# One more held pair in each down product, a longer allowance for the weights behind a norm, norm pieces by list, first loads on two queues

## The chip, the cores and the metric

The kernel runs on one core of a Trainium2 chip. The metric is the device time of one execution, in microseconds (us). The engines are named as in the profile: PE multiplies matrices, DVE works on vectors, ACT casts and evaluates functions, POOL is the general one, SP issues most of the DMAs. PEld is the loading of weights into PE.

## The reference, cut to what matters

A single decoder layer for 256 tokens of width 2048, in float32:

```
h = layer_norm(alpha*h + 0.5*swiglu(h, w_ffn1_gu, w_ffn1_down))     # norm 1
... = split(h @ w_in)          # retention, attention, gates
h = layer_norm(alpha*h + mixed @ w_mix_out)                         # norm 2
h = layer_norm(alpha*h + 0.5*swiglu(h, w_ffn2_gu, w_ffn2_down))     # norm 3
h = layer_norm(alpha*h + sigmoid(h @ w_ple_gate) * (p @ w_ple_proj))

swiglu(x, w_gu, w_down): g, u = split(x @ w_gu);  (silu(g) * u) @ w_down
```

The inner width of swiglu is 5632. A layer_norm needs the sum over a whole row, so no product behind a norm can start on a token before the product ahead of it has finished for that token in all 2048 columns.

## The kernel before

**Numbers.** Each float32 operand is carried as two parts that PE multiplies fast: a high part, which ACT casts (L93), and a low part, which DVE gets by subtraction (L94). A product is three matmuls: low × high, high × high, high × low (L302 to L304).

**Weights.** A weight arrives in chunks of 512 KB: a raw load by SP (L109), a high part on ACT, a low part on DVE. `plan` lists all units (one chunk, or two for a scheme with seven products in place of eight) in the order of use. `fill` (L188) is called whenever a unit is done: it makes the next loaded unit if the ready ones amount to less than `ahead` (a sum of the units' times) and there are slots, and asks for the next load if all of it is below `far`. `quiet(True)` stops the making, not the loading. `slots_for_weights` sets slots, `ahead` and `far`. 46 slots of 4 KB for each partition are shared with everything else.

**The order.** The program runs the first feed-forward block f1 (`ffn`, L762), norm 1, the mixers (L975), norm 2, the second feed-forward block f2, norm 3, the embedding (L1337) and the last norm. Each engine does its instructions in the order in which the code writes them. A feed-forward block has gate and up products, and then the down product in two halves of 1024 columns each, d0 and d1.

**What is held back.** The two token halves t = 0 and t = 1 of 128 tokens each are normalised one after the other. So that PE has work meanwhile, the last pairs of chunks ahead of a norm are held back (`HELD_PAIRS`, 2 for f1 and 3 for f2; `HELD_MIX` 4 chunks ahead of norm 2). `held_out` (L433) first runs t = 0 of all held steps (a pair is two steps, one for each 512 columns; a step is six matmuls for each t), then `normal(0)`, which DVE works on while PE runs t = 1 of the same steps, in half-steps of three matmuls. In the last `calm` steps of the t = 0 pass, and after it, `fill` is quiet. Ahead of norm 1 two blocks of w_pp follow (`put_by`, L646), ahead of norm 2 two more; of those a count is six matmuls.

**The norm.** `Norm` (L528): `columns(t, n)` adds a product to the residual (L911) and takes its statistics (L541); `normal(t)` does that for the last 512 columns, works out mean and deviation, and normalises the first 512 columns in two halves (L512, L513); `more(t, c)` normalises piece c of 512 columns. `turn(t, c)` asks for `more(t, c+1)`, unless that is the piece `put_off`, and has PE transpose piece c (L520), ACT cast it and DVE subtract: this gives `ht`, the input of the next product. The lists of events, like

```
events = ((8, (0, 0)), (10, (0, 1)), (11, (0, 2)), (12, "make"), (12, "make"), (12, "sums"))
```

say after how many half-steps of t = 1 a piece (t, c) is turned, a unit is made, or `normal(1)` is done ("sums"). After the norm `first` (L604) does the same for the next product: t = 0 of its first `FRONT` chunks (w_rv behind norm 1, w_pg behind norm 3; `FRONT_PAIRS` pairs of gate and up chunks behind norm 2), then t = 1, with events that turn the pieces of t = 1 and do the put-off one ("more"), and end the quiet ("go").

**The start.** `warm_up` (L1504) has PE transpose an identity 16 times while the first loads come. `load_x_chunk(0)` (L1474) loads the first quarter of x in three pieces and the first two units in two pieces each, all on SP's queue.

Of the kernel before, what the change touches and what calls it, by code (L numbers as in the profile page):

```python
# [23 lines left out]
LN_EPS = 1e-5  # L24
GN_EPS = 1e-5
KD = D // P
# [2 lines left out]

HELD_MIX = 4  # L30
FRONT = 6

WARM = 16
FRONT_PAIRS = 3
HELD_PAIRS = 2, 3
SLOTS = 46


# [12 lines left out]
def layer(ctx: ExitStack, tc: tile.TileContext, io):  # L51
# [44 lines left out]
    class Chunk:  # L96


        def __init__(self, key, pieces=1, queue=None, between=None):
            src = chunk_of(key)  # L100
            self.key, self.paired = key, key[0].endswith("_gu") or key[0][-1] == "2"
            self.name = "_".join(map(str, key))
            self.raw = slot(list(src.shape), F32, "r" + self.name)
            n = src.shape[2] // pieces
            self.parts = [slice(j * n, j * n + n) for j in range(pieces)]
            for j, at in enumerate(self.parts):
                if between is not None and j:
                    between()
                (queue or sync).dma_start(self.raw[:, :, at], src[:, :, at])  # L109

        def make_hi(self):
# [416 lines left out]
    class Norm:  # L528
# [23 lines left out]

        def turn(self, t, c):

            args = self.y, t, self.i, self.new
            if c < 3 and (t, c + 1) != self.put_off:
                self.more(t, c + 1)
            if c == 0:
                for k0 in (0, 2):
                    ln_turn(*args, k0, 2, self.keep.get(c))  # L560
            else:
                ln_turn(*args, 4 * c, 4, self.keep.get(c))

        def follow(self, n, events):

# [196 lines left out]
    def ffn(name, i, ht, norm, keep, residual, keepers, away):  # L762
# [28 lines left out]
        for j in range(KF // 4):  # L791
            pg, pu = banks(f"{name}g{j}"), banks(f"{name}u{j}")
            units = gu_units(j)
            plain = len(units) - sum(kind == "S" for kind, p in units)
            n_of = {(0, 0): KD, (0, 1): KD, (1, 0): KD, (1, 1): KD}
            for kind, p in units:
                if kind == "S":
                    for at in ((0, 0), (0, 1), (1, 0)):
                        n_of[at] -= 1
                    n_of[1, 1] -= 2  # L800
            sums = [[Sum((pg, pu)[n][t], n_of[t, n]) for n in range(2)] for t in range(2)]
            got = []

            if norm is not None and j == 0:
                front, units = units[:FRONT_PAIRS], units[FRONT_PAIRS:]
                steps = [(gu_keys(name, 0)(n, p), 2 * p, n) for _, p in front for n in range(2)]
                norm.first(steps, rhs, sums, (
                    (3, (1, 0)), (5, (1, 1)), (6, "more"), (7, (0, 2)), (8, (1, 2)), (9, (0, 3)), (10, (1, 3)), (10, "go"),
                ))
                slots_for_weights(24)  # L810

            def before(u, j=j, offset=KD // 2 - len(units)):
                u += offset
                if j == 0 and norm is None and u % 2 == 0:
                    first_chunk(u // 2)
                    if u == 6:
                        slots_for_weights(24)
                    if u == 2:
                        load_constants()
                if j == 0 and u == 7:  # L820
                    for g in sorted({p // 2 for p in SEVEN}):
                        hi, lo = (slot([P, 8, P], F32R, f"{name}f{w}{g}") for w in "hl")
                        made[g] = seven_forms(keep[g], hi, lo)
                if j == KF // 4 - 1 and u in (4, 6):
                    convert(u // 2 - 2)

            block(f"{name}{j}", units, gu_keys(name, j), rhs, forms, sums, lambda *a: got.extend(seven_common(*a)), before)
            if got:
                g, v = got
                for x, ps in ((g, pg), (v, pu)):  # L830
                    for t in range(2):
                        dve.tensor_tensor(x[:, t], x[:, t], ps[t], ALU.add)  # L832
                act.activation(g, g, AF.Silu)  # L833
                dve.tensor_tensor(v, g, v, ALU.mult)
            else:
                v = slot([P, 2, 512], F32, f"{name}v{j}")
                for t in range(2):
                    act.activation(v[:, t], pg[t], AF.Silu)
                for t in range(2):
                    dve.tensor_tensor(v[:, t], v[:, t], pu[t], ALU.mult)  # L840
            later(2, lambda j=j, v=v: turned(j, v))
# [44 lines left out]
            block_stats(stats, y, n)  # L886


        last_ahead = 136
        last = {}  # L890
        for at, (kind, p) in enumerate(second + [("P", p) for p in held]):
            last[p // 2] = at
# [11 lines left out]
        pt_ = [banks(f"{name}e{t}") for t in range(2)]  # L904
        sums = [[Sum(pt_[t][n], n_of[1][t, n]) for n in range(2)] for t in range(2)]
        block(f"{name}d1", second, down_keys(name, 1), lhs, forms, sums, fold(1), before_unit)
        slots_for_weights(27, last_ahead, last_ahead + 24)
        steps = [(down_keys(name, 1)(n, p), 2 * p, n) for n in range(2) for p in held]

        def combine(sl, p):  # L910
# [1 line left out]

        norm = Norm((2, 3), sums, combine, y, stats, i, 4 * LN_EPS, keepers, away, (0, 3))
        if i < 2:
            events = ((8, (0, 0)), (10, (0, 1)), (11, (0, 2)), (12, "make"), (12, "make"), (12, "sums"))
            norm.run(steps, lhs, events, (0, 1), 4)
        else:
            norm.run(steps, lhs, ((8, (0, 0)), (11, (0, 1))))
        return norm


# [53 lines left out]
    def mixers(ht, norm, residual, keepers, away):  # L975
# [353 lines left out]
            done(u)  # L1329
            run_side()  # L1330
        steps = [(("w_mix", 3, c), 2 * c, 0) for c in range(first, KD // 2)]
        norm = Norm((3,), sums, combine, y, stats, 1, LN_EPS, keepers, away, (0, 2))
        norm.run(steps, lhs, ((8, (0, 0)), (10, (0, 1)), (10, "sums")), (2, 3))
        return norm

# [1 line left out]
    def embedding(ht, norm, y):  # L1337
# [77 lines left out]
        for blk in range(4):  # L1415
            pgs = banks(f"pg{blk}")
            sums = [Sum(b, KD) for b in pgs]
            sg = slot([P, 2, 512], F32, f"sg{blk}")
            key = ("w_pg", blk)
            if blk == 0:  # L1420
                for j in range(4):
                    pp[j] = load_columns(pp, j, "ppr")
                steps = [(key + (c,), 2 * c, 0) for c in range(FRONT)]
                norm.first(steps, lhs, [[s] for s in sums], (
                    (1, (0, 2)), (1, "sums"), (6, (1, 0)), (7, (1, 1)), (8, (1, 2)), (8, "more"), (9, (1, 3)),
                    (10, (0, 3)), (10, "go"),
                ))
                slots_for_weights(24)
                for c in range(FRONT, KD // 2):
                    u = take(key + (c,))  # L1430
                    tokens_chunk(u.chunk, 2 * c, lhs, sums, (0, 1))
                    done(u)
            elif blk < 3:
                for c in range(KD // 2):
                    u = take(key + (c,))
                    tokens_chunk(u.chunk, 2 * c, lhs, sums, (0, 1))
                    done(u)
                    run_side()
            if blk < 3:
                finish(blk, pgs[0], sg, 0)  # L1440
                later(1, lambda blk=blk, pgs=pgs, sg=sg: finish(blk, pgs[1], sg, 1))
                if blk == 0:
                    g, b = ln_vectors(3)
                    two_rows = small.tile([P, 96], F32, tag="plnm", bufs=1, name="plnm")
                    pool.memset(two_rows, 0.0)
                    ident_r = small.tile([P, P], F32R, tag="identr", bufs=1, name="identr")
                    act.copy(ident_r, ident)
                if blk == 1:
                    later(3, rows_of_vectors)
                    later(4, lambda: scale(0))  # L1450
                    later(6, lambda: scale(1))
                if blk == 2:
                    later(6, lambda: scale(2))
                continue

            def first_done():
                finish(3, pgs[0], sg, 0)
                first_half(*ln_stats(stats[:, 0], 3, 0, LN_EPS))

            steps = [(key + (c,), 2 * c, 0) for c in range(KD // 2)]  # L1460
            held_out(steps, lhs, [[s] for s in sums], lambda t, j: None, first_done, lambda n: None, 0)
            last_half()
# [11 lines left out]
    def load_x_chunk(c):  # L1474
# [4 lines left out]
            split_x(c, slice(0, 4))  # L1479
            return  # L1480
        parts = [slice(0, 1), slice(1, 2), slice(2, 4)]
        load = lambda at: sync.dma_start(raw[:, at], io["xT"][c][:, at])
        load(parts[0])
        for j in range(2):
            u = plan.pop(0)
            u.load(pieces=2, queue=sync, between=lambda: load(parts[1]) if j == 0 else None)
            u.chunk.make_hi()
            room["used"] += u.keeps
            ready.append(u)
        load(parts[2])  # L1490
        first, second = (u.chunk for u in ready)
        split_x(c, parts[0])
        first.make_part(first.parts[0])
# [134 lines left out]
```

## Time and profile before

| | |
|---|---|
| median of 3 runs | 2289.36 us (2289.07 to 2289.7) |
| profiled execution, its own time | 2290.82 us |
| span of that execution | 2288.6 us |
| mean granted TensorE clock | 0.998 |
| ACT busy | 1189.9 us (52%) |
| DMA | 465.88 MB, mean 204 GB/s |

The span runs from the first to the last instruction. A line of the timeline has the start in us, the duration, the engine with the line of the code, the operation, output and inputs, sizes, and how many instructions it stands for (x4); in brackets the idle time of the engine ahead of it and what ended that. A matmul's duration covers its passage through the array; the pace is the distance between starts.

### The profile page before, as it was taken

Reading aid. Unit: us, or ns where it says so; the run is one execution under the profiler, and the core shown is the slowest. Engines: PE = TensorE matmul, PEld = TensorE weight load, DVE = VectorE, ACT = ScalarE, POOL = GpSimd, SP = SyncE. Lnnn points to the kernel's source line nnn. Section 1 sums busy time; section 2 is a strip of 40 time slices with the busy share of each in tenths; the row PEclk is TensorE's granted clock in tenths of the full one; section 3 lists DMA queues with packets and bytes.
Section 4 is the critical chain, followed back from the end, with each engine's and each line's share of the span. In section 5 each row is a group of like instructions: output and inputs, shape, how many; then the busy total and the mean of one; then the engine's idle time right before and its main releaser. Section 6 shows DMA issues by size and latency. Waiting matters only on the chain.

```text
span 2288.6 us, 28866 instructions
## 1 busy us (share of the span) xinstructions
PE 2273.1 (99%) x10492; PEld 1887.0 (82%) x10492; DVE 1948.2 (85%) x2474; ACT 1189.9 (52%) x1438; POOL 97.0 (4%) x56
## 2 busy tenths in 40 slices
PE   9999999999999999999999999999999999999998
PEld 8888888888888888888778888888888888888876
DVE  6999999999988885677789786779999999889877
ACT  5555555556554342435556454355565555555533
POOL 0000000000000530124000000000000000000000
PEclk9999999999999999999999999999999999999999
DMA  8666665665577565545447567566656566565772
GB/s 298 202 204 196 199 210 178 209 198 193 215 280 282 175 224 164 171 161 166 138 152 244 170 218 279 191 226 207 195 191 205 184 203 217 179 221 193 276 258 74
DMA packets 194022, 465.88 MB, mean 204 GB/s; under 512 B 14796, under 2 KB 16460, under 8 KB 193880
## 3 DMA queue, kind: packets, MB, share of 16 engines
q1 hardware_dynamic: 192296, 461.73, 60.9%
q10 hardware_dynamic: 1584, 2.31, 0.4%
q8 instruction: 82, 1.34, 0.2%
q14 instruction: 60, 0.49, 0.1%
HBM read 455.60 MB, written 8.39 MB: 203 GB/s over the span
## 4 chain that ended last, share of the span: by engine, by line
PE 97%; DVE 2%; DMA 0%; issue 0%; ACT 0%; SPq 0%; ACTq 0%
PE f1g L302 3%; PE f1g L304 3%; PE f1g L303 3%; PE f2g L304 3%; PE f2g L302 3%; PE f2g L303 3%; PE rqk L253 3%; PE f1u L304 2%; PE f1u L302 2%; PE f1u L303 2%; PE f2u L304 2%; PE f2u L302 2%; PE f2u L303 2%; PE aqk L253 2%; PE f1d L302 2%; PE f2d L302 2%
## 5 line engine op out<-in xcount | busy, mean ns | idle before, releaser
L94 DVE TENSOR_TENSOR lf_gu<-rf_gu,hf_gu 128x1024 fp32r<-128x1024 f32 (+1 forms) x284 | 334.4, 1211 | 16.2 <-ACT hf_gu L93 15.4
L93 ACT CAST hf_gu<-rf_gu 128x1024 fp32r<-128x1024 f32 (+1 forms) x284 | 282.2, 1043 | 22.3 <-DMA rf_gu<-in_f_gu 20.5
L94 DVE TENSOR_TENSOR lw_in_f<-rw_in_f,hw_in_f 128x1024 fp32r<-128x1024 f32 x140 | 195.6, 1427 | 29.4 <-ACT hw_in_f L93 26.9
L94 DVE TENSOR_TENSOR lf_down<-rf_down,hf_down 128x1024 fp32r<-128x1024 f32 x152 | 181.1, 1220 | 23.1 <-ACT hf_down L93 20.3
L93 ACT CAST hf_down<-rf_down 128x1024 fp32r<-128x1024 f32 x152 | 155.4, 1050 | 75.8 <-DMA rf_down<-in_f_down 21.9
L93 ACT CAST huf_gu<-uf_gu 128x1024 fp32r<-128x1024 f32 x70 | 73.8, 1054 | 156.4 <-DVE uf_gu L168 153.5
L93 ACT CAST hw_in_f<-rw_in_f 128x1024 fp32r<-128x1024 f32 x140 | 138.8, 1051 | 3.2 <-DMA rw_in_f<-in_w_in_f 2.9
L302 PE MATMUL f1g<-hf_gu,xt 128*128 128x512 f32 x247 | 97.2, 393 | 0.5 <-ACT hf_gu L93 0.5
L304 PE MATMUL f1g<-lf_gu,xt 128*128 128x512 f32 x247 | 96.9, 392 | 0.0
L303 PE MATMUL f1g<-hf_gu,xt 128*128 128x512 f32 x247 | 96.9, 392 | 0.0
L302 PE MATMUL f2g<-hf_gu,ht 128*128 128x512 f32 x247 | 96.4, 390 | 0.0
L304 PE MATMUL f2g<-lf_gu,ht 128*128 128x512 f32 x247 | 96.2, 390 | 0.0
L303 PE MATMUL f2g<-hf_gu,ht 128*128 128x512 f32 x247 | 96.2, 389 | 0.0
L93 ACT CAST hvf_gu<-vf_gu 128x1024 fp32r<-128x1024 f32 x70 | 73.8, 1054 | 30.2 <-DVE vf_gu L170 29.5
L833 ACT ACTIVATE eve<-eve 128x1024 f32<-128x1024 f32 x20 | 21.2, 1062 | 124.5 <-DVE eve L832 124.5
L94 DVE TENSOR_TENSOR luf_gu<-uf_gu,huf_gu 128x1024 fp32r<-128x1024 f32 x70 | 85.3, 1218 | 0.0
L94 DVE TENSOR_TENSOR lvf_gu<-vf_gu,hvf_gu 128x1024 fp32r<-128x1024 f32 x70 | 85.3, 1218 | 0.0
L302 PE MATMUL f2u<-hf_gu,ht 128*128 128x512 f32 x212 | 83.8, 395 | 0.0
L302 PE MATMUL f1u<-hf_gu,xt 128*128 128x512 f32 x212 | 83.4, 394 | 0.0
L304 PE MATMUL f2u<-lf_gu,ht 128*128 128x512 f32 x212 | 82.6, 390 | 0.0
L303 PE MATMUL f2u<-hf_gu,ht 128*128 128x512 f32 x212 | 82.6, 390 | 0.0
L303 PE MATMUL f1u<-hf_gu,xt 128*128 128x512 f32 x212 | 82.6, 390 | 0.0
(1358 smaller groups left out, 6452.5 us busy)
## 6 DMA issues: line engine op xcount, KB each, us to landing
rf_gu<-in_f_gu SPq DMA_DIRECT2D x350, 512.0 KB
rf_down<-in_f_down SPq DMA_DIRECT2D x176, 512.0 KB
rw_in_f<-in_w_in_f SPq DMA_DIRECT2D x148, 512.0 KB
rw_rv<-in_w_rv SPq DMA_DIRECT2D x32, 512.0 KB
rw_ret<-in_w_ret SPq DMA_DIRECT2D x32, 512.0 KB
rw_mix<-in_w_mix SPq DMA_DIRECT2D x32, 512.0 KB
rw_pg<-in_w_pg SPq DMA_DIRECT2D x32, 512.0 KB
rw_att<-in_w_att SPq DMA_DIRECT2D x16, 512.0 KB
```

Source lines behind the costliest of these rows:

```text
L93: act.copy(dst_hi, src)
L94: (lo_engine or dve).tensor_tensor(dst_lo, src, dst_hi, ALU.subtract)
L253: pe.matmul(ps[f], hi[:, kk, f * P : (f + 1) * P], rhs(k), start=k == 0, stop=k == n_k - 1,)
L302: pe.matmul(o, al, bh, start=first, stop=False)
L303: pe.matmul(o, ah, bh, start=False, stop=False)
L304: pe.matmul(o, ah, bl, start=False, stop=self.left == 0)
L833: act.activation(g, g, AF.Silu)
```

## The change

- `HELD_PAIRS` goes from 2, 3 to 3, 4: f1 and f2 hold back one pair more ahead of norms 1 and 3, and the events are counted anew. Piece (0,2) of norm 3 and its "sums" move from the embedding's list to the end of the held steps.
- The allowance `last_ahead` behind a down product goes from 136 to 160 (f1) and 150 (f2), with `far` 24 above it as before, and the slots from 27 to 30.
- Behind norm 3, five chunks of w_pg (`FRONT_LAST`) instead of six run by halves.
- Norm 2 puts off no piece; "more" leaves its list. In norms with a put-off piece, `turn(1, 0)` writes `more(1, 1)` behind the transposes and parts of (1,0) instead of ahead of them.
- 19 warm transposes instead of 16; the three loads of x are issued first on SP's queue, the first unit's two loads on ACT's queue, the second unit's on SP's.

```
-WARM = 16
+FRONT_LAST = 5
+WARM = 19
-HELD_PAIRS = 2, 3
+HELD_PAIRS = 3, 4
...
-        def __init__(self, key, pieces=1, queue=None, between=None):
+        def __init__(self, key, pieces=1, queue=None):
...
-            for j, at in enumerate(self.parts):
-                if between is not None and j:
-                    between()
+            for at in self.parts:
                 (queue or sync).dma_start(self.raw[:, :, at], src[:, :, at])
...
         def turn(self, t, c):
             args = self.y, t, self.i, self.new
-            if c < 3 and (t, c + 1) != self.put_off:
+            at_once = (t, c) == (1, 0) and self.put_off is not None
+            following = c < 3 and (t, c + 1) != self.put_off
+            if following and not at_once:
                 self.more(t, c + 1)
             if c == 0:
                 for k0 in (0, 2):
                     ln_turn(*args, k0, 2, self.keep.get(c))
             else:
                 ln_turn(*args, 4 * c, 4, self.keep.get(c))
+            if following and at_once:
+                self.more(t, c + 1)
...
-                    (3, (1, 0)), (5, (1, 1)), (6, "more"), (7, (0, 2)), (8, (1, 2)), (9, (0, 3)), (10, (1, 3)), (10, "go"),
+                    (3, (1, 0)), (5, (1, 1)), (7, (0, 2)), (8, (1, 2)), (9, (0, 3)), (10, (1, 3)), (10, "go"),
...
-        last_ahead = 136
+        last_ahead = 160 if i < 2 else 150
...
-        slots_for_weights(27, last_ahead, last_ahead + 24)
+        slots_for_weights(30, last_ahead, last_ahead + 24)
...
-            events = ((8, (0, 0)), (10, (0, 1)), (11, (0, 2)), (12, "make"), (12, "make"), (12, "sums"))
+            events = ((11, (0, 0)), (13, (0, 1)), (15, (0, 2)), (15, "make"), (15, "make"), (15, "sums"))
             norm.run(steps, lhs, events, (0, 1), 4)
         else:
-            norm.run(steps, lhs, ((8, (0, 0)), (11, (0, 1))))
+            norm.run(steps, lhs, ((10, (0, 0)), (13, (0, 1)), (16, (0, 2)), (16, "sums")))
...
-        norm = Norm((3,), sums, combine, y, stats, 1, LN_EPS, keepers, away, (0, 2))
+        norm = Norm((3,), sums, combine, y, stats, 1, LN_EPS, keepers, away, None)
...
-                steps = [(key + (c,), 2 * c, 0) for c in range(FRONT)]
+                steps = [(key + (c,), 2 * c, 0) for c in range(FRONT_LAST)]
                 norm.first(steps, lhs, [[s] for s in sums], (
-                    (1, (0, 2)), (1, "sums"), (6, (1, 0)), (7, (1, 1)), (8, (1, 2)), (8, "more"), (9, (1, 3)),
-                    (10, (0, 3)), (10, "go"),
+                    (5, (1, 0)), (6, (1, 1)), (7, (1, 2)), (7, "more"), (8, (1, 3)), (9, (0, 3)), (9, "go"),
                 ))
...
-        load = lambda at: sync.dma_start(raw[:, at], io["xT"][c][:, at])
-        load(parts[0])
-        for j in range(2):
+        for at in parts:
+            sync.dma_start(raw[:, at], io["xT"][c][:, at])
+        for queue in (act, sync):
             u = plan.pop(0)
-            u.load(pieces=2, queue=sync, between=lambda: load(parts[1]) if j == 0 else None)
+            u.load(pieces=2, queue=queue)
...
-        load(parts[2])
```

More of the change, by code (lines that the diff above doesn't have):

```diff
@@ L1422, in embedding @@
                     pp[j] = load_columns(pp, j, "ppr")
-                steps = [(key + (c,), 2 * c, 0) for c in range(FRONT)]
+                steps = [(key + (c,), 2 * c, 0) for c in range(FRONT_LAST)]
                 norm.first(steps, lhs, [[s] for s in sums], (
-                    (1, (0, 2)), (1, "sums"), (6, (1, 0)), (7, (1, 1)), (8, (1, 2)), (8, "more"), (9, (1, 3)),
-                    (10, (0, 3)), (10, "go"),
+                    (5, (1, 0)), (6, (1, 1)), (7, (1, 2)), (7, "more"), (8, (1, 3)), (9, (0, 3)), (9, "go"),
                 ))
                 slots_for_weights(24)
-                for c in range(FRONT, KD // 2):
+                for c in range(FRONT_LAST, KD // 2):
                     u = take(key + (c,))
```

## Prediction

> **What bounds the kernel now.** I read the page's head first, then the waits of PE, then the timelines around the three norms and the start.
>
> ```profile
> span 2288.6 us, 28866 instructions
> PE 2273.1 (99%) x10492; PEld 1887.0 (82%) x10492; DVE 1948.2 (85%) x2474; ACT 1189.9 (52%) x1438; POOL 97.0 (4%) x56
> ```
>
> PE is busy for all but 15.5 us of the span. The matmuls, PE's work, are the same in number after the change, so only idle time of PE, and time at a lower clock, can come or go.
>
> ```profile
> PE lnps L520 <- DVE f2y L513: 1.7, 2, 1.2
> PE pg L302 <- DVE ht L94: 1.1, 1, 1.1
> PE lnps L520 <- DVE mixy L513: 1.1, 2, 0.8
> PE lnps L520 <- DVE f1y L513: 0.8, 2, 0.5
> PE f1g L302 <- ACT hf_gu L93: 0.5, 1, 0.5
> ```
>
> The columns are total us, times, longest. Those five are what the change can reach: 5.2 us, nearly all of it PE waiting for DVE to normalise a piece (L512, L513) that PE then transposes (L520). The end of the kernel is not touched. Beside these waits stands a stretch at half clock:
>
> ```profile
> 717.00:720.40 3.40, 2.63 (x14) 1.73 (x14) 3.29 (x8) 0.74 (x2) 0.00 (x0) 1.00 0.96 365
> 2177.25:2180.66 3.41, 1.76 (x10) 1.05 (x9) 3.17 (x10) 0.53 (x2) 0.00 (x0) 1.00 0.94 310
> 2180.66:2184.07 3.41, 3.41 (x11) 2.52 (x10) 3.37 (x6) 0.21 (x1) 0.00 (x0) 0.50 1.03 419
> ```
>
> These are stretches of the windows view: length, busy time of PE, weight load, DVE, ACT, POOL, then granted clock. After a window in which PE was busy 1.76 of 3.41 us the clock was 0.50 for the next; after one with 2.63 it was not.
>
> **Where the numbers stand.** The profiled execution took 2290.82 us, 2.2 beyond its span, and lies 1.46 above the median of the runs, 2289.36. The sum is made against the profiled execution and carried over to the median.
>
> **Norm 1** (f1's down product, three pairs held back where there were two).
>
> ```profile
> 683.14 1.23 DVE L94 TENSOR_TENSOR lf_down<-rf_down,hf_down 128x1024 fp32r<-128x1024 f32 x1 [0.40 <-ACT hf_down L93]
> 691.74 4.62 DVE L94 TENSOR_TENSOR lw_rv<-rw_rv,hw_rv 128x1024 fp32r<-128x1024 f32 x4
> 696.28 0.68 DVE L94 TENSOR_TENSOR pt<-praw,pt 128x512 fp32r<-128x512 f32 x1
> 696.88 0.68 DVE L911 TENSOR_TENSOR f1y<-f1y,f1e 128x512 f32<-128x512 f32 x1
> 702.29 0.48 DVE L513 SCALAR_TENSOR_TENSOR f1y<-f1y,rstd,ln_b 128x256 f32<-128x256 f32 x1
> 703.21 0.48 DVE L513 SCALAR_TENSOR_TENSOR f1y<-f1y,rstd,ln_b 128x256 f32<-128x256 f32 x1
> 705.71 0.75 DVE L513 SCALAR_TENSOR_TENSOR f1y<-f1y,rstd,ln_b 128x512 f32<-128x512 f32 x1
> 698.17 0.39 PE L302 MATMUL f1e<-hf_down,f1al 128*128 128x512 f32 x1
> 703.61 0.60 PE L520 MATMUL lnps<-ident,f1y 128*128 128x128 f32 x4
> 718.62 0.41 PE L520 MATMUL lnps<-ident,f1y 128*128 128x128 f32 x2 [0.51 <-DVE f1y L513]
> 719.17 0.75 DVE L513 SCALAR_TENSOR_TENSOR f1y<-f1y,rstd,ln_b 128x512 f32<-128x512 f32 x1
> 719.84 0.75 DVE L94 TENSOR_TENSOR ht<-lnps,ht 128x256 fp32r<-128x256 f32 x2
> 720.26 0.60 PE L520 MATMUL lnps<-ident,f1y 128*128 128x128 f32 x4
> ```
>
> PE. The first token half of all held chunks runs, then the second. 24 matmuls start from 698.17 to 703.61, 0.2267 us each. One more pair is two more steps. Their 24 matmuls leave the plain part, and 12 come back in the first half, so the first half ends 12 × 0.2267 = 2.72 us sooner: the second half starts at 698.17 − 2.72 = 695.45 and the first piece, due after 33 of its matmuls, at 695.45 + 7.48 = 702.93.
>
> DVE. It works without a gap from 683.14. In the order of the changed program six low parts of w_rv (not four) and pt stand before the first L911: steps 1 and 2 of six are no longer quiet, and the larger allowance lets two more units be made. Each takes 4.62 / 4 less the overlap, 1.135, so the first L911 comes at 696.88 + 2.27 = 699.15; loads asked for sooner can close at most the 0.40 us before 683.14, and I take all of it: 698.75. In before, piece (0,0) was ready in two halves, at 702.77 and 703.69, which is 5.89 and 6.81 after the first L911. So they come at 704.64 and 705.56. With the 0.13 and 0.06 us from ready to start that the rows at norm 3 below show, PE goes on at 704.77, 1.84 late, and after 0.19 of transposes waits 0.66 more: **2.5**. Bounds: 0 if the lows are made in time, 2.9 with nothing of the 0.40 regained.
>
> Piece (0,1) is asked for 9 matmuls later (2.04 and 0.2 for the transposes); DVE has the columns of the second half and its two L512/L513 before it, 706.46 − 703.69 = 2.77 in before. 2.77 + 0.1 against 2.4 gives **0.45**. Then nothing is late until the second half's norm, where 0.8 was waited in two pieces before and is again. What is new there: the list puts L512/L513 of piece (1,1) behind both lows of (1,0), where before they stood ahead of them (719.17 before 719.84). The lows wait for transposes that start at 718.62 and for ACT, and end at 719.84 + 0.75 = 720.59 at the earliest; 1.53 behind them is 722.1 where PE came at 720.26. Two transposes of cover are taken off, and the delay of the lows in before was the pieces ahead of them, so they start some 0.8 sooner: **1.0** (0 to 1.9).
>
> The three make **+3.95**. At norm 3 below, 1.40 and 0.58 late were 1.24 and 0.42 of idle, so 2.5 late is some 2.2 of idle within 2.6 us. A window of 3.4 us that holds it all has PE busy for 1.2, below the 1.76 after which the clock was 0.50. At half clock 3.4 us hold 8 matmuls at 0.427 and lose 8 × 0.2 = 1.6; the 0.45 of piece (0,1) is hidden in it. So **+1.15** more. The windows go on whatever PE does, so a wait of 2.2 can also be cut in two: then no window falls below 1.76. I take it as whole, since 1.7 of it is one wait; both are kept.
>
> A rule speaks against the halving. The Trainium skill, "TensorE: Matmul & The Clock Gate", section "HAM oscillation — how this bites in real kernels", gives the rule as "no PE-idle gaps >~3.4µs"; by it no wait here would halve the clock, and the term would be 0. The trace differs: the longest idle in the window before the halving was 1.2 us. The case without it is rival B.
>
> **Norm 2** (no piece put off).
>
> ```profile
> 1478.87 0.69 DVE L94 TENSOR_TENSOR ht<-keep,ht 128x512 fp32r<-128x512 f32 x1 [2.73 <-ACT ht L93]
> 1492.07 0.66 PE L520 MATMUL lnps<-ident,mixy 128*128 128x128 f32 x4 [0.79 <-DVE mixy L513]
> ```
>
> The L512/L513 of piece (0,2), 1.5 us, move from just before 1492.07 into DVE's 2.73 idle before 1478.87. The wait of 0.79, 0.95 counted from start to start, goes; the next piece was already normalised. **−0.95** (0 if ACT is late).
>
> **Norm 3** (four pairs; five chunks of w_pg in front instead of six).
>
> ```profile
> 2167.48 3.49 DVE L94 TENSOR_TENSOR lw_pg<-rw_pg,hw_pg 128x1024 fp32r<-128x1024 f32 x3
> 2172.19 1.23 DVE L94 TENSOR_TENSOR lw_pg<-rw_pg,hw_pg 128x1024 fp32r<-128x1024 f32 x1 [1.22 <-ACT hw_pg L93]
> 2173.34 0.68 DVE L911 TENSOR_TENSOR f2y<-f2y,f2e 128x512 f32<-128x512 f32 x1
> 2179.49 0.48 DVE L513 SCALAR_TENSOR_TENSOR f2y<-f2y,rstd,ln_b 128x256 f32<-128x256 f32 x1
> 2172.36 0.39 PE L302 MATMUL f2e<-hf_down,f2al 128*128 128x512 f32 x1
> 2177.57 0.39 PE L304 MATMUL f2e<-lf_down,f2ah 128*128 128x512 f32 x1
> 2179.20 0.41 PE L520 MATMUL lnps<-ident,f2y 128*128 128x128 f32 x2 [1.24 <-DVE f2y L513]
> 2180.03 0.44 PE L520 MATMUL lnps<-ident,f2y 128*128 128x128 f32 x2 [0.42 <-DVE f2y L513]
> ```
>
> The sixth low of w_pg, which waited 1.22 for its load, no longer stands before the norm: the first L911 comes at 2170.9, 2.44 sooner, and the last quarter of (0,0) at 2179.97 − 2.44 = 2177.53. PE's second half starts at 2172.36 − 2.72 = 2169.64 and asks after 30 matmuls, at 2176.44: 0.32 + 0.66 = 0.98 of waiting, against 1.40 + 0.58 before, and too little to halve the clock. Before: 1.98 + 1.6 at half clock + 1.28 (the wait on ht) = 4.86. After: 0.98, 0.5 at (0,1) as in norm 1, 0.95 on ht, 0.35 at (1,1), whose pieces now stand behind the lows, and 1.0 for the sixth chunk, made only when the last piece is turned, with one step (6 matmuls, 1.36) to cover the ACT cast and the 1.23 of the low (0.4 to 1.2): 3.78. **−1.1** (−3.9 if nothing is late, +0.5 if the clock halves).
>
> **Start.**
>
> ```profile
> 2.80:6.20 3.40, 2.90 (x13) 2.34 (x11) 1.10 (x3) 1.33 (x3) 0.00 (x0) 1.00 0.89 274
> 1.18 0.42 SPq L109 DMA_DIRECT2D rf_gu<-in_f_gu  x1
> 2.03 0.20 ACT L1513 ACTIVATE warm<-warm 128x1 f32<-128x1 f32 x1
> 5.54 0.80 PE L302 MATMUL f1g<-hf_gu,xt 128*128 128x512 f32 x1 [0.50 <-ACT hf_gu L93]
> 12.00 1.23 DVE L94 TENSOR_TENSOR lf_gu<-rf_gu,hf_gu 128x1024 fp32r<-128x1024 f32 x1 [1.24 <-ACT hf_gu L93]
> 13.54 0.39 PE L304 MATMUL f1g<-lf_gu,xt 128*128 128x512 f32 x1
> 20.66 0.39 ACTq L680 DMA_DIRECT2D cst<-in_cst  x1
> ```
>
> The first chunk's two loads go to ACT's queue, behind the ACTIVATE that ends at 2.23, so up to 1.05 later than 1.18; SP's later loads move up two issues of 0.42. Three more warm transposes fill the 0.50 gap ahead of 5.54. Worst: first matmul 1.05 later at half clock, +0.9. Best: the gap closed, a half-clock window of 1 us less, but the matmul at 13.54 needs the low that ends at 13.23, 0.3 before it: −0.8. I take **0**, between them, since the cast of the first chunk waits for its DMA and not for an issue.
>
> The Trainium skill, "DMA: Bandwidth & Descriptors", section "Issuing engines are not separate DMA queues", says that loads issued by two engines share the same 16 DMA engines and only the issue time is gained. By it the gain is at most those issues; the trace of before cannot show it.
>
> **Sum.** 3.95 + 1.15 − 0.95 − 1.1 + 0 = +3.05: the profiled execution comes to 2293.9, the median to **2292.4**. The loads asked for sooner I cost at nothing: matmuls on chunks that are already made hide them. The DMA share is 0.94 to 1.03 in the windows above, so if one lands late for that, the price is a wait like the 1.22 at 2172.19.
>
> **Rivals.** About 0.2%, 4.6 us, is what a measurement of this kernel can tell from no change: 2284.8 to 2293.9.
> - **A, forecast**, 42%: 2292.4.
> - **B**, the same without the halving at norm 1, 16%: 2291.2. For it: 2.63 of 3.40 did not halve. Against: 1.7 of idle in one wait.
> - **C**, DVE in time at norm 1, because the lows are made before the fold at 686.83 instead of behind it, 14%: the waits of (0,0) and (0,1) go, 1.0 stays: 1.0 − 0.95 − 1.1 = −1.05, 2288.3. Against: DVE has no gap there to make them in.
> - **D**, slower, 20%: the second half of norm 1 halves the clock too. Before, its window had 2.63 of 3.40; 1.0 more idle brings it to about 1.65, just below 1.76, the point from which it decides. Price 1.6, and up to 1.2 for the same at norm 3: 2294.0 to 2295.2, middle 2294.6.
> - **E**, faster, 8%: the change does what a longer second half would, all pieces in time at norm 3 (−3.9), start −0.8, norm 2 −0.95, norm 1 +1.0: 2284.7.
>
> The range takes in A, B, D and the lower side of C: 2287.0 to 2295.3; E and the upper edge of D stay out. Faster 0.07 (E, part), slower 0.21 (D and a tail of A), same 0.72.
>
> **What would show it.** Norm 1: a wait of about 2 us at L520 for f1y, six lows of w_rv ahead of the first L911 at about 699, a new wait of 1 us at (1,1), clock 0.50 once. Norm 2: one wait left, 0.3. Norm 3: no half clock, first L911 at about 2171 on before's scale, waits of PE on ht and on lw_pg. The prediction is wrong if f1y keeps a wait of 0.8 or if DVE has a gap before norm 1.

## The result and the profile after

The changed kernel takes 2297.52 us (median of 6 runs, 2296.95 to 2298.77); the kernel before took 2289.27 beside it. The ratio is 1.0037, with a 95% interval of 1.0025 to 1.005: slower, by 8.2 us. The forecast was 2292.4, and its range ended at 2295.3.

The head of the page, and the waits of PE (total us, times, longest):

```profile
span 2295.0 us, 28860 instructions
PE 2274.3 (99%) x10495; PEld 1885.3 (82%) x10495; DVE 1948.9 (85%) x2474; ACT 1191.0 (52%) x1438; POOL 97.3 (4%) x56
```

```profile
PE lnps L519 <- DVE f1y L512: 7.3, 5, 5.4
PE lnps L519 <- DVE f2y L512: 1.2, 4, 0.4
PE pg L301 <- DVE ht L95: 0.7, 1, 0.7
PE pg L303 <- DVE lw_pg L95: 0.5, 1, 0.5
PE lnps L519 <- DVE mixy L512: 0.3, 1, 0.3
PE pg L301 <- ACT hw_pg L94: 0.2, 1, 0.2
```

The change moves the code: L302 to L304 of before are L301 to L303, L520 is L519, L513 is L512, L94 (the low part) is L95, L93 (the cast) is L94, L911 is L915. The wait on mixy fell from 1.1 to 0.3 and the wait on ht from 1.1 to 0.7, as forecast; those on w_pg are the forecast ones of the sixth chunk. The wait on f1y, 0.8 in before, is 7.3, and one of its pieces alone is 5.4.

That piece is (0,0) of norm 1. Its DVE, ACT and PE rows in the timeline:

```profile
690.25 3.49 DVE L95 TENSOR_TENSOR lw_rv<-rw_rv,hw_rv 128x1024 fp32r<-128x1024 f32 x3
693.65 0.68 DVE L95 TENSOR_TENSOR pt<-praw,pt 128x512 fp32r<-128x512 f32 x1
697.69 3.50 DVE L95 TENSOR_TENSOR lw_rv<-rw_rv,hw_rv 128x1024 fp32r<-128x1024 f32 x3 [3.35 <-ACT hw_rv L94]
701.10 0.68 DVE L915 TENSOR_TENSOR f1y<-f1y,f1e 128x512 f32<-128x512 f32 x1
690.81 0.61 ACT L94 CAST pt<-praw 128x512 fp32r<-128x512 f32 x1
696.60 2.00 ACT L94 CAST hw_rv<-rw_rv 128x1024 fp32r<-128x1024 f32 x2 [5.18 <-PE f1e L302]
698.77 1.05 ACT L94 CAST hw_rv<-rw_rv 128x1024 fp32r<-128x1024 f32 x1 [0.17 <-DMA rw_rv<-in_w_rv]
695.23 0.80 SPq L108 DMA_DIRECT2D rw_rv<-in_w_rv  x2
693.91 0.39 PE L301 MATMUL f1e<-hf_down,f1al 128*128 128x512 f32 x1
706.95 0.66 PE L519 MATMUL lnps<-ident,f1y 128*128 128x128 f32 x2 [5.40 <-DVE f1y L512]
707.78 0.69 PE L519 MATMUL lnps<-ident,f1y 128*128 128x128 f32 x2 [0.17 <-DVE f1y L512]
```

All six lows do stand ahead of the first L915, as forecast. But DVE does not make them in a row. It stands for 3.35 us behind pt, because ACT has not cast the fourth chunk, and ACT stands for 5.18 us, and what releases it is PE, a matmul of the down product. The second half of the held steps starts at 693.91; a step in it is 6 matmuls, 1.36 us. ACT goes on 2.69 later, when two steps are done, and SP issues the next two loads of w_rv, the sixth chunk's first, 1.32 later, when one is. So cast and loads wait until held chunks are done with: what they wait for is their slots. It is not a load: for most of the time in which ACT stands, 691.42 to 696.60, no transfer runs at all (the last two numbers of a line of the windows view are the DMA share and GB/s).

```profile
691.90:695.30 3.40, 3.40 (x17) 2.82 (x16) 2.44 (x3) 0.00 (x0) 0.00 (x0) 1.00 0.00 0
```

Start, clock and the rest of norm 1, in the windows view (length, busy time of PE, PEld, DVE, ACT, POOL, granted clock) and PE's timeline:

```profile
2.80:6.20 3.40, 3.40 (x17) 2.99 (x16) 1.43 (x3) 1.33 (x3) 0.00 (x0) 1.00 1.04 324
6.20:9.60 3.40, 3.40 (x14) 2.21 (x14) 2.54 (x5) 2.69 (x5) 0.00 (x0) 1.00 1.06 372
701.51:704.93 3.42, 0.04 (x1) 0.00 (x0) 3.18 (x9) 0.00 (x0) 0.00 (x0) 1.00 0.95 381
704.93:708.34 3.41, 1.22 (x5) 0.85 (x6) 3.18 (x10) 0.37 (x1) 0.00 (x0) 0.50 0.00 0
708.34:711.75 3.41, 3.41 (x10) 2.64 (x10) 3.36 (x6) 0.37 (x1) 0.00 (x0) 0.50 0.02 5
```

```profile
725.11 0.41 PE L519 MATMUL lnps<-ident,f1y 128*128 128x128 f32 x2 [0.51 <-DVE f1y L512]
727.97 0.63 PE L519 MATMUL lnps<-ident,f1y 128*128 128x128 f32 x4 [1.06 <-DVE f1y L512]
```

The clock was 0.50 for two windows behind the long wait, and piece (1,1), at 727.97, has the new wait of 1.06 idle.

From here on a wait is often counted from start to start: the distance between the starts of two matmuls, less what it is without a wait. That is somewhat more than the idle time in brackets.

By position in the two profiles the parts are these. The second half of the held steps at norm 1 starts at 693.91 instead of 695.45 (698.17 less the 12 matmuls): the start gave 1.54. Piece (1,1) comes at 727.97 instead of 720.26, so norm 1 cost 7.71 + 1.54 = **9.25**. Norm 2 gave 0.95. Behind norm 3 the last stage stands 6.1 later than in before, so norm 3 gave 0.7 by position (its waits alone fell by 1.0), and 0.3 came at the very end: the 6.4 us between the spans. The medians differ by 8.2, since the profiled execution of before lay 1.5 above its median; why is seen below.

### The profile page after: what moved, and what is told of

Read it like the earlier page. It is cut to its first block, busy times and chain, and to the rows that moved or that the text cites. A ratio compares the mean times of both kernels' runs of the same rounds, so it can differ in the third digit from the quotient of the medians.

```text
span 2295.0 us, 28860 instructions
## 1 busy us (share of the span) xinstructions
PE 2274.3 (99%) x10495; PEld 1885.3 (82%) x10495; DVE 1948.9 (85%) x2474; ACT 1191.0 (52%) x1438; POOL 97.3 (4%) x56
## 4 chain that ended last, share of the span: by engine, by line
PE 97%; DVE 2%; DMA 0%; issue 0%; ACT 0%; SPq 0%; POOL 0%; DVEq 0%; POOLq 0%
PE f1g L303 3%; PE f1g L301 3%; PE f1g L302 3%; PE f2g L301 3%; PE f2g L303 3%; PE f2g L302 3%; PE rqk L252 3%; PE f1u L302 2%; PE f1u L301 2%; PE f1u L303 2%; PE f2u L301 2%; PE f2u L302 2%; PE f2u L303 2%; PE aqk L252 2%; PE f2d L302 2%; PE f1d L301 2%
## 5 line engine op out<-in xcount | busy, mean ns | idle before, releaser
L95 DVE TENSOR_TENSOR lf_gu<-rf_gu,hf_gu 128x1024 fp32r<-128x1024 f32 (+1 forms) x284 | 334.6, 1210 | 15.3 <-ACT hf_gu L94 14.4
L94 ACT CAST hf_gu<-rf_gu 128x1024 fp32r<-128x1024 f32 (+1 forms) x284 | 282.4, 1043 | 21.5 <-DMA rf_gu<-in_f_gu 21.3
L95 DVE TENSOR_TENSOR lw_in_f<-rw_in_f,hw_in_f 128x1024 fp32r<-128x1024 f32 x140 | 195.7, 1427 | 29.7 <-ACT hw_in_f L94 27.1
L95 DVE TENSOR_TENSOR lf_down<-rf_down,hf_down 128x1024 fp32r<-128x1024 f32 x152 | 181.2, 1219 | 25.2 <-ACT hf_down L94 22.3
L94 ACT CAST hf_down<-rf_down 128x1024 fp32r<-128x1024 f32 x152 | 155.4, 1050 | 78.1 <-DMA rf_down<-in_f_down 22.7
L94 ACT CAST huf_gu<-uf_gu 128x1024 fp32r<-128x1024 f32 x70 | 73.8, 1054 | 157.1 <-DVE uf_gu L167 154.2
L94 ACT CAST hw_in_f<-rw_in_f 128x1024 fp32r<-128x1024 f32 x140 | 138.8, 1051 | 1.5 <-PE ga0a L302 0.7
L303 PE MATMUL f1g<-lf_gu,xt 128*128 128x512 f32 x247 | 96.4, 390 | 0.0
L301 PE MATMUL f1g<-hf_gu,xt 128*128 128x512 f32 x247 | 96.3, 390 | 0.0
L301 PE MATMUL f2g<-hf_gu,ht 128*128 128x512 f32 x247 | 96.3, 390 | 0.0
L303 PE MATMUL f2g<-lf_gu,ht 128*128 128x512 f32 x247 | 96.2, 389 | 0.0
L302 PE MATMUL f2g<-hf_gu,ht 128*128 128x512 f32 x247 | 96.1, 389 | 0.0
L302 PE MATMUL f1g<-hf_gu,xt 128*128 128x512 f32 x247 | 96.1, 389 | 0.0
L94 ACT CAST hvf_gu<-vf_gu 128x1024 fp32r<-128x1024 f32 x70 | 73.8, 1055 | 29.6 <-DVE vf_gu L169 28.6
L95 DVE TENSOR_TENSOR luf_gu<-uf_gu,huf_gu 128x1024 fp32r<-128x1024 f32 x70 | 85.2, 1217 | 0.0
L95 DVE TENSOR_TENSOR lvf_gu<-vf_gu,hvf_gu 128x1024 fp32r<-128x1024 f32 x70 | 85.2, 1217 | 0.0
L301 PE MATMUL f2u<-hf_gu,ht 128*128 128x512 f32 x212 | 83.7, 395 | 0.0
L301 PE MATMUL f1u<-hf_gu,xt 128*128 128x512 f32 x212 | 83.3, 393 | 0.0
L303 PE MATMUL f2u<-lf_gu,ht 128*128 128x512 f32 x212 | 82.6, 390 | 0.0
L302 PE MATMUL f2u<-hf_gu,ht 128*128 128x512 f32 x212 | 82.6, 389 | 0.0
L302 PE MATMUL f1u<-hf_gu,xt 128*128 128x512 f32 x212 | 82.5, 389 | 0.0
```

Of the source, the lines that this page charges most:

```text
L94: act.copy(dst_hi, src)
L95: (lo_engine or dve).tensor_tensor(dst_lo, src, dst_hi, ALU.subtract)
L301: pe.matmul(o, al, bh, start=first, stop=False)
L302: pe.matmul(o, ah, bh, start=False, stop=False)
L303: pe.matmul(o, ah, bl, start=False, stop=self.left == 0)
```

## The experiments

Two theories stood for the wait at (0,0), with the forecast's own as a third. **S**: the longer allowance has loads and casts of w_rv asked for when no slot is free, and DVE's norm work is queued behind them. **L**: a load landed late. **W**: the two added lows as work on DVE are the whole of it. Each run is beside the kernel before on the same chip: 2289.71 in the first four, 2289.54 in the next, 2289.0 in the last three.

| run | edit | us | before |
|---|---|---|---|
| e1 | changed kernel, 27 slots in f1 | 2293.47 | 2289.71 |
| e2 | changed kernel, allowance 136 in f1 | 2292.32 | 2289.71 |
| e3 | changed kernel, more(1,1) first at norm 1 | 2296.36 | 2289.71 |
| e4 | before + norm 2 | 2288.39 | 2289.71 |
| e5 | before + 19 warm transposes | 2289.34 | 2289.54 |
| e6 | before + loads on two queues | 2288.11 | 2289.54 |
| e7 | before + norm 3 | 2290.61 | 2289.54 |
| e8 | before + whole start | 2288.09 (one run) | 2289.54 |
| e9 | changed kernel without norm 1's part | 2288.62 | 2289.0 |
| e10 | before + start + norm 2 | 2286.72 | 2289.0 |
| e11 | e10 + sixth low of w_pg later | 2285.57 | 2289.0 |

**e1: slots for weights at 27 again, in f1.**

```
-        slots_for_weights(30, last_ahead, last_ahead + 24)
+        slots_for_weights(27 if i < 2 else 30, last_ahead, last_ahead + 24)
```

> The changed kernel with the slots for weights behind f1's down product at 27 again; nothing else is undone. Theory S (the making of w_rv chunks ahead of norm 1 runs out of slots, and ACT and DVE stand until a held chunk is done): by the order of the instructions only three w_rv chunks are made ahead of norm 1 and none waits for a slot of a held chunk, so the first L915 comes at about 694 and the wait for piece (0,0), 5.4 + 0.17 idle, goes, and the half clock behind it too: 6.05 + 2.0 less. The three missing chunks are made later, 0 to 2.5 us of waits on lw_rv or hw_rv. Time 2289.5 to 2292. Rival L (the waits are those of loads landing late): the wait for f1y stays above 3 us, 2294 or more.

The DVE rows of norm 1, and then PE's where the w_rv product takes the chunks:

```profile
693.10 0.68 DVE L95 TENSOR_TENSOR pt<-praw,pt 128x512 fp32r<-128x512 f32 x1
693.70 0.68 DVE L915 TENSOR_TENSOR f1y<-f1y,f1e 128x512 f32<-128x512 f32 x1
701.30 0.60 PE L519 MATMUL lnps<-ident,f1y 128*128 128x128 f32 x4
718.77 0.79 PE L301 MATMUL rv<-hw_rv,ht 128*128 128x512 f32 x1 [1.41 <-ACT hw_rv L94]
720.87 0.80 PE L303 MATMUL rv<-lw_rv,ht 128*128 128x512 f32 x1 [0.88 <-DVE lw_rv L95]
```

The first L915 follows pt at once, 7.4 us sooner than in the changed kernel, and PE turns all four parts of (0,0) at 701.30 without waiting. The time fell by 4.05 to 2293.47, less than expected: the chunks that were not made ahead of the norm are now awaited behind it, 1.41 on a cast and 0.88 on a low, 3.9 us from start to start, and behind these waits the clock is halved as well, for two windows:

```profile
715.20:718.62 3.42, 1.43 (x7) 0.59 (x5) 2.77 (x7) 1.59 (x3) 0.00 (x0) 1.00 0.99 352
718.62:722.03 3.41, 2.38 (x5) 1.47 (x6) 3.34 (x5) 0.10 (x1) 0.00 (x0) 0.50 1.03 378
722.03:725.44 3.41, 3.41 (x12) 2.73 (x11) 1.22 (x3) 0.59 (x1) 0.00 (x0) 0.50 0.99 347
```

S holds on the wait; its estimate of what comes after was too low, and the half clock, which it expected to go, came at another place. L's number did not come (2294 or more, f1y above 3), but with only three chunks of w_rv ahead of the norm a late load of the others could not have held it here either. What speaks against L is the window without a transfer above, and e2.

**e2: allowance at 136 again, slots at 30.**

```
-        last_ahead = 160 if i < 2 else 150
+        last_ahead = 136 if i < 2 else 150
```

> The changed kernel with the allowance behind f1's down product at 136 again, the slots left at 30. Four w_rv chunks are made ahead of norm 1, the fourth behind pt; the sixth, whose load landed last, is not among them. Theory S: the cast of the fourth waits for the slot of the first held chunk, free 1.36 us after the second half begins, one step sooner than in the changed kernel; then cast and low take 2.3, and the wait for piece (0,0) is 2.8 counted from start to start; whether the clock still halves is open: 2292.5 to 2294.5. Rival L: only the sixth chunk's late load mattered, the wait is below 0.7, no half clock: 2289.5 to 2290.5. Rival W (the work of the two added lows on DVE alone, as predicted, 2.5): two lows fewer leave less than 0.3.

ACT's and DVE's rows at the fourth chunk, PE's first matmul of the second half and its transposes, and two windows:

```profile
695.19 1.05 ACT L94 CAST hw_rv<-rw_rv 128x1024 fp32r<-128x1024 f32 x1 [3.76 <-PE f1e L302]
696.27 1.23 DVE L95 TENSOR_TENSOR lw_rv<-rw_rv,hw_rv 128x1024 fp32r<-128x1024 f32 x1 [2.23 <-ACT hw_rv L94]
697.41 0.68 DVE L915 TENSOR_TENSOR f1y<-f1y,f1e 128x512 f32<-128x512 f32 x1
693.86 0.39 PE L301 MATMUL f1e<-hf_down,f1al 128*128 128x512 f32 x1
703.28 0.41 PE L519 MATMUL lnps<-ident,f1y 128*128 128x128 f32 x2 [1.78 <-DVE f1y L512]
704.10 0.44 PE L519 MATMUL lnps<-ident,f1y 128*128 128x128 f32 x2 [0.42 <-DVE f1y L512]
```

```profile
701.77:705.19 3.42, 1.50 (x8) 1.16 (x9) 3.28 (x8) 0.75 (x2) 0.00 (x0) 1.00 0.12 47
705.19:708.60 3.41, 3.41 (x12) 2.71 (x11) 3.34 (x7) 0.00 (x0) 0.00 (x0) 0.50 0.02 5
```

The cast starts 1.33 us behind the start of the second half, one step, where it was 2.69, two steps. The wait at (0,0) is 2.52 from start to start (1.94 + 0.58; expected 2.8, with W less than 0.3), and the clock still went down. As in the changed kernel no transfer runs just before the cast (DMA share 0.00 from 693 to 696). The time is 2292.32, just below the expected 2292.5 to 2294.5. Two doses of one cause, one step and two, give what S says of each. L is out, and so is W as the whole cause; in the changed kernel the two added lows still cost DVE the 2.27 us that the prediction gave them, on top of the wait for slots.

**e3: more(1,1) ahead of the transposes again, at norm 1 alone.**

```
-            at_once = (t, c) == (1, 0) and self.put_off is not None
+            at_once = (t, c) == (1, 0) and self.i == 2
```

> The changed kernel with more(1,1) of norm 1 written ahead of the transposes of (1,0) again; norm 3 keeps the new order. Theory: the new wait of 1.06 idle (1.23 from start to start) at piece (1,1) of norm 1 goes and nothing takes its place: 2296.3. Rival: the lows of (1,0), now later, are awaited by the w_rv matmuls instead and 0 is gained: 2297.5. The wait of 5.4 at (0,0) stays in both.

2296.36. The 5.4 stays, and PE turns (1,1) with no idle noted where it waited 1.06:

```profile
725.75 0.41 PE L519 MATMUL lnps<-ident,f1y 128*128 128x128 f32 x2 [0.51 <-DVE f1y L512]
727.39 0.60 PE L519 MATMUL lnps<-ident,f1y 128*128 128x128 f32 x4
```

**e4: the edit of norm 2 alone** (`put_off` None, "more" out of its list).

> The kernel before with the edit of norm 2 alone: no piece put off, no 'more' in its list. Theory: the wait of 0.79 at piece (0,2) goes, 0.95 from start to start, the 0.3 at (1,0) stays: 2288.3. Rival: the two instructions delay the sums of t=1 and the first wait grows by as much: 2289.3. Its start is that of the kernel before: if the half clock up to 9.6 us shows in this profile as well, the start's part is not chance of one execution.

2288.39 beside 2289.71, ratio 0.9994 (0.9985 to 1.0003). The 0.95 is gone from the trace and nothing replaces it. This run told more by what it left alone. At norm 3 it has the code of before, but no half clock: the wait at (0,0) is 0.67 + 0.58 from start to start instead of 1.40 + 0.58. And at the start the clock was full from 4.32 us on, in the profile of before only from 9.78 (last section), but PE then waited 0.81 + 0.70 for gate and up chunks, so that norm 1 came only 0.09 sooner.

**e5, e6, e8: the start in parts** (`WARM = 19`; the loads as in the diff; both). The label of e8 names norm 2, which that kernel leaves as it was.

The W of these three is another than that of e2.

> The kernel before with 19 warm transposes and nothing else. Theory Q (the start's gain of 1.54 us in the changed kernel comes from the loads: x issued at once, two issues taken off SP): the clock may be full a window sooner, but then PE waits for the second gate and up chunks as in the kernel with norm 2's edit alone (0.81 + 0.70 at 11 and 12.4 us), so the shift at norm 1 (first transposes of t=1, 717.70 in the kernel before) is within 0.3 of 0: 2289.5. Rival W (the gap of 0.5 ahead of the first matmul kept the clock at half): the shift is -1.5: 2288.1.

> The kernel before with the loads on two queues as in the changed kernel, 16 warm transposes. Theory Q: the second chunks land as soon as in the changed kernel, so the shift at norm 1 is -1.0 to -1.5 even if one window runs at half clock: 2288.3. Rival W: with the gap of about 0.5 ahead of the first matmul the half clock stays and the shift is above -0.5: 2289.5.

> The kernel before with the whole start of the changed kernel (two queues and 19 warm transposes). Both theories: the shift at norm 1 is -1.5, and the two parts add up or one of them has it all.

The start of the last w_rv matmul ahead of piece (1,0) at norm 1 is a common mark. It stands at 717.05, 716.96 and 717.54 in the three profiles with the old start (before, e4, e7); at 716.31 with the warm transposes alone, 716.15 with the queues alone, 715.61 with both. Against the mean of the three, 717.18, that is -0.9, -1.0 and -1.6. By the mark each part alone gives more than half of what both give. But each is one profile, profiles with the same start differ by 0.6, and the profiled execution of e5, 2288.56, is the second fastest of its eleven (median 2289.34). The times are what Q expected of both, 2289.34 and 2288.11 (Q 2289.5 and 2288.3, W 2288.1 and 2289.5), though neither differs from before beyond its interval (e5 1.0001, 0.9992 to 1.001; e6 0.9995, 0.9986 to 1.0004). And in e4 a clock that was full sooner moved the mark by 0.09. So the loads have most of the evidence; how the gain divides between the two parts stays open.

**e7: the edits of norm 3 alone.**

```
-HELD_PAIRS = 2, 3
+FRONT_LAST = 5
+HELD_PAIRS = 2, 4
...
+            at_once = (t, c) == (1, 0) and self.i == 2
...
-        last_ahead = 136
+        last_ahead = 136 if i < 2 else 150
...
-        slots_for_weights(27, last_ahead, last_ahead + 24)
+        slots_for_weights(27 if i < 2 else 30, last_ahead, last_ahead + 24)
```

with the two lists of norm 3 as in the change. In this kernel every line of the view stands one further on than in before (L521 for L520).

> The kernel before with the edits of norm 3 alone: four pairs held in f2, five w_pg chunks in front, allowance 150 and 30 slots there, more(1,1) behind the lows of (1,0) there. Its waits in the changed kernel made 3.85 us (1.11 at (0,0), 0.41 at (0,1), 0.86 on ht, 0.37 at (1,1), 1.10 on the sixth chunk). Theory H (the half clock at norm 3 in the profile of before is chance of that execution, as the kernel with norm 2's edit alone shows none there): most executions of before pay 2.9 there, so this part costs 0.9: 2290.5. Rival (as predicted, -1.1): 2288.6.

```profile
PE lnps L521 <- DVE f2y L514: 1.1, 4, 0.4
PE pg L303 <- DVE ht L95: 0.7, 1, 0.7
PE pg L305 <- DVE lw_pg L95: 0.5, 1, 0.5
PE pg L303 <- ACT hw_pg L94: 0.2, 1, 0.2
```

2290.61, 1.07 above before (ratio 1.0006, 0.9997 to 1.0015). The waits, 3.70 from start to start, are those of the changed kernel (3.85). What they replace varies: with the code of before, norm 3 cost 4.86 in the profile of before, and 2.93, 3.34, 3.78, 3.27 and 2.27 in e4, e5, e6, e8 and e10, by how long the sixth low had to wait for its cast (1.22 idle in before; 0.56, 1.08, 1.52, 0.69 and 0 in the others). Only the first has the half clock. This agrees with H, and the last section shows what the chance is; the interval of the time alone would not decide it.

**e9, e10: all but norm 1; and start with norm 2.** e9 takes the changed kernel and undoes what concerns norm 1:

```
-HELD_PAIRS = 3, 4
+HELD_PAIRS = 2, 4
...
-            events = ((11, (0, 0)), (13, (0, 1)), (15, (0, 2)), (15, "make"), (15, "make"), (15, "sums"))
+            events = ((8, (0, 0)), (10, (0, 1)), (11, (0, 2)), (12, "make"), (12, "make"), (12, "sums"))
```

and the edits of e1, e2 and e3 with it. e10 is before with the start and the edit of norm 2.

> The changed kernel with all that concerns norm 1 undone: two held pairs in f1, its old events, 136 and 27 there, more(1,1) ahead of the lows there. Start, norm 2 and norm 3 stay as changed. Theory (norm 1 costs 9.25 by the trace, the rest gains: start 1.5, norm 2 0.95, and loses 0.4 at norm 3 against an execution of before without the half clock there): 2289.5 - 1.5 - 0.95 + 0.4 = 2287.5. Rival (the parts of the prediction, norm 3 -1.1): 2286.0. If the slowdown were spread over the parts: above 2290.

> The kernel before with the changed start and the edit of norm 2, norms 1 and 3 as before. Theory: -1.5 and -0.95 add up: 2287.1, 0.4 below the kernel with the norm 3 part. Rival (norm 3's part gains 1.1): it stays 1.1 above that kernel.

2288.62 and 2286.72, 1.1 above and 0.4 below what was expected. Without norm 1's part the changed kernel is 8.9 us faster (8.6 when each is set against the kernel before beside it) and no slower than before (ratio 1.0, 0.9991 to 1.0009): the slowdown is norm 1's. And norm 3's part costs 1.9 between these two, not 0.4. e10 beats before: 0.999 (0.9981 to 0.9999).

**e11: at norm 3, only the sixth low moved.** To e10:

```
-        last_ahead = 136
+        last_ahead = 136 if i < 2 else 124
...
-        slots_for_weights(27, last_ahead, last_ahead + 24)
+        slots_for_weights(27, last_ahead, 160)
...
-                    (1, (0, 2)), (1, "sums"), (6, (1, 0)), (7, (1, 1)), (8, (1, 2)), (8, "more"), (9, (1, 3)),
+                    (1, "make"), (1, (0, 2)), (1, "sums"), (6, (1, 0)), (7, (1, 1)), (8, (1, 2)), (8, "more"), (9, (1, 3)),
```

> The kernel before with the changed start, the edit of norm 2, and at norm 3 only the sixth low of w_pg moved: allowance 124 there, and the chunk is made by an event ahead of piece (0,2), in DVE's idle time between the lows of (0,1) and (0,2). Three pairs held and six chunks in front as before. Theory: the first L911 of norm 3 no longer waits for the load of the sixth chunk, the 0.7 to 1.5 + 0.58 waited at (0,0) fall to below 0.3; 0.41 at (0,1) and 1.28 on ht stay: 1.5 less than the kernel with start and norm 2 alone, 2285.6. Rival: the low in DVE's idle time delays the low of (0,2) or the sums of t=1, and PE waits as much there: 2287.1.

```profile
2181.03 1.22 DVE L94 TENSOR_TENSOR lw_pg<-rw_pg,hw_pg 128x1024 fp32r<-128x1024 f32 x1
2182.29 0.69 DVE L94 TENSOR_TENSOR ht<-lnps,ht 128x512 fp32r<-128x512 f32 x1
```

```profile
PE lnps L520 <- DVE f2y L513: 0.2, 1, 0.2
PE pg L302 <- DVE ht L94: 1.1, 1, 1.1
```

2285.57, ratio to before 0.9986 (0.9977 to 0.9994), the fastest of all. The sixth low lies between two lows of ht, and the waits on f2y fell to 0.2. It is 1.15 below e10, whose profile happened to have the smallest wait of its kind.

## Why the prediction was wrong

The direction of the sum was right and its size was not: +3.05 forecast, +8.2 measured, outside the range.

Norm 1 cost 9.25 where 5.1 was forecast (3.95 and 1.15), norm 3 cost 0.7 where it was to gain 1.1, and the start gained 1.3 where 0 was forecast.

- **Norm 1, piece (0,0): the step that failed.** "It works without a gap from 683.14 ... six low parts ... stand before the first L911 ... Each takes ... 1.135." The order was right, the time was not: the three last lows are behind a cast that waits for a slot. Carried back by the 1.54 of the start, the first L915 was due at 697.2 and came at 701.10, 3.9 later. DVE's idle row has 3.35 of it; a gap of DVE before norm 1 is what the prediction itself named as a sign of being wrong. Most of the rest is that nothing of the 0.40 was regained: the lows of w_rv begin at 690.25, and 691.74 less 1.54 is 690.20. The wait was 6.05 from start to start (5.56 + 0.49) instead of 2.5. The allowance was costed as if a longer one could only bring loads sooner ("The loads asked for sooner I cost at nothing"). It also takes slots: e1 and e2 set it back, in slots or in allowance, and the wait is 0 and 2.52.
- **Piece (0,1)**: no wait of its own (0.45 forecast), because matmuls at half clock covered it.
- **The half clock** came. What norm 1 cost beyond its waits is 9.25 - 6.05 - 1.2 = 2.0, where 1.6 was forecast (1.15 and the 0.45): the wait reached into a second window, so the clock was low for two.
- **Piece (1,1)**: 1.23 from start to start, forecast 1.0; e3's median is 1.16 lower.
- **Norm 2**: -0.95, as forecast.
- **Norm 3**: the waits were 3.85, forecast 3.78, piece by piece within 0.2. The other side of the subtraction failed: 1.6 of half clock in the profile of before was taken as what every execution pays. Five further profiles of the same code have none, and their mean is 3.1 where 4.86 was taken. So the part costs about 0.7 by the waits, 1.1 by e7 and 1.9 by e9 against e10, and does not gain 1.1.
- **Carrying the sum to the median**: the same slip again. The profiled execution lay 1.46 above the median, and the same 1.46 was taken off both. But the change removes the very half clock that it had.
- **Start**: 0 forecast, -1.54 in the profile, -0.9 to -1.6 by the mark in the others with the whole start. The bound of 0.3 before the low at 13.23 held the loads fixed; with the queues changed that chunk's low starts at 10.37 instead of 12.00. In the times it shows beyond the interval only together with norm 2, in e10 and e11.
- **The rivals**: slower was given 0.21 and came, but D's mechanism, a second half clock at (1,0), did not: the window there has PE busy for 2.35, not 1.65, and the clock stayed at 1.00. C, DVE in time, is what e1 makes, and then the chunks of w_rv are late.
- **The rule on idle gaps** that the prediction quotes from the Trainium skill ("TensorE: Matmul & The Clock Gate", "HAM oscillation — how this bites in real kernels"), "no PE-idle gaps >~3.4µs": the 5.40 here is beyond it and the clock fell, but it also fell in e2 with 1.78 and 0.42 idle. The trace disagrees with the rule.
- **My own bound** of 1.76 busy of 3.41 is about right, if the windows are those of the clock itself (last section); the prediction had said that they can cut a wait in two, and could not tell where.
- **The two queues**: e6 gains 1.0 by the mark, beside 0.84 for two of SP's issues of 0.42, and the mark scatters by 0.6. That does not contradict the Trainium skill, "DMA: Bandwidth & Descriptors", "Issuing engines are not separate DMA queues", by which only issue time is gained.

For the medians the terms are: start -1.3 (the mean over e8 to e11 and the changed kernel: 1.6, 1.4, 0.9, 1.3 and 1.5), norm 1 +9.25, norm 2 -0.95, norm 3 +0.7, together +7.7 of the 8.2 measured.

## What to carry to other kernels

A longer allowance for prefetching is a claim on buffers as well as on time: where a pool is nearly full, count the slots that each asked load and cast takes, and look at what is queued behind the instruction that would wait for the next free one. Work ahead of a critical piece on the same engine should only be such as can be done without waiting, and e11 shows the other use of that: one low part moved to a place where its engine is idle anyway.
Before a difference is taken from one profile, look whether its execution has an event that others lack, such as a stretch at half clock.

## What the runs showed of the hardware

The clock is set in windows of its own, and the trace shows where they lie. In the records of the clock that each of the thirteen traces holds, it changes only at times that are whole multiples of 3.413 us apart; the windows view, asked in steps of 0.01 us, shows the time of a change. In the changed kernel it changes at 704.93, 711.75 and 2288.71 (2 and 462 windows between them), in before at 2180.66, 2184.07 and 2283.06 (1 and 29). Where the windows begin differs from trace to trace. In e6 the clock changes at 2280.60, so 31 windows before it one begins at 2174.79:

```profile
2174.79:2178.20 3.41, 2.20 (x10) 1.50 (x8) 3.06 (x13) 0.00 (x0) 0.00 (x0) 1.00 0.77 290
2178.20:2181.62 3.42, 2.85 (x13) 1.99 (x13) 3.31 (x7) 0.74 (x2) 0.00 (x0) 1.00 1.02 412
```

Norm 3 was later in e6 (1.52 + 0.58) than in before (1.40 + 0.58), and yet the clock stayed at 1.00. The longer wait of e6, 1.36 idle, ends at 2178.35, so a new window begins inside it, and PE is busy for 2.20 in the one and 2.85 in the other. In before one window holds both waits, with 1.76. On these windows, over all traces, the full clock was halved after PE had been busy for 0.00 to 1.50 us, and after 1.76; it was kept after 1.72 (e5, near its end) and after everything from 1.79 up. So in this kernel the edge lies near 1.75 of 3.41, about as sharply as PE's busy time can say, in which the ends of the matmuls are modelled; and whether a wait of 2 us costs a half clock depends on where the windows fall in that execution.

At the start the column of the granted clock does not show the half clock: before has 1.00 in this window, and yet 10 matmuls where the changed kernel has 14, and one takes 0.63 there, against 0.40 in the changed kernel. The first change of the clock that the traces hold is at 9.78 us in before and at 5.19 in the changed kernel, and ahead of it the column reads 1.00:

```profile
6.20:9.60 3.40, 3.40 (x10) 2.67 (x9) 2.17 (x5) 2.05 (x4) 0.00 (x0) 1.00 0.97 310
7.84 0.63 PE L304 MATMUL f1g<-lf_gu,xt 128*128 128x512 f32 x1
```

```profile
8.14 0.40 PE L301 MATMUL f1g<-hf_gu,xt 128*128 128x512 f32 x1
```
